# A hybrid Hyena and attention encoder layer: convolutions in two stages, attention chained behind its hyena, an early first operand

## The chip, the cores and the metric

The kernel runs on one core of one Trainium2 chip. The metric is the device time of one execution in microseconds (us). The time before is 3018.79 us, the median of 3 runs (3017.01 to 3024.18).

## The reference

Two independent sequences (prompt, s = 0, and sample, s = 1) of T = 1024 tokens with model width D = 1024 go through one encoder layer in fp32, with a final RMS norm.

```python
h = rmsnorm(x, norm1_g)
u_h, q, k, v, g_h, g_a = split(h @ w_in)        # 1536, 512, 128, 128, 1024, 1024
y_h = hyena_mixer(u_h, ...)                     # z = gate * (fftconv(z, filt[o]) + bias[o] * z), o = 0, 1
y_a = window_attention(rope(q), rope(k), v)     # blocks of 128, window 128, a sink logit
merged = sigmoid(g_h) * (y_h @ w_up_hyena) + sigmoid(g_a) * (y_a @ w_up_attn)
x = x + merged @ w_out
h = rmsnorm(x, norm2_g)
x = x + (silu(h @ w_ff_gate) * (h @ w_ff_up)) @ w_ff_down
return rmsnorm(x, final_g)
```

There are 8 query heads and 2 key heads of 64, and the feed-forward width is 2816. The convolutions are bidirectional ones of length 2T over 512 channels, two of them (o = 0 and 1) for each sequence.

## The kernel before

**Numbers.** A large product keeps fp32 accuracy by splitting each operand into a high and a low fp32r part (`part`, L338 to L342: ScalarE casts, L341, and VectorE subtracts, L342) and doing three matmuls: high·high, high·low, low·high. In the projections these are L559, L560, L561, in the feed-forward part L1045, L1046, L1047.

**Stages.** `main` runs, for each sequence, the projections that feed the hyena (`proj_u`), q, k and v (`proj_qkv`) and the gates (`proj_gates`), sequence 0 first, all in pool `pa`. Then in pool `pb` come the merges: `merge_up(s, i)`, the hyena's (i = 0) and the attention's (i = 1) up products, weighted by the gates (loads of the intermediate results L917, of the gates L922), and `merge_out`, the product with w_out and the residual. Last come the feed-forward halves `ffn_up` and `ffn_down`, in Strassen form (`strassen`, seven products instead of eight). Before `ffn_up(0)`, `b_side(k)` makes for each of four quarters k of the contraction the seven operands B11, T1, T2, B21, T3, B22, T4 out of the normed rows.

**What runs beside what.** Hyena and attention are a side stream: generators that yield the cost of each step. `mix(main, side, rate)` takes a step of the main stream (10.4 for a column block of a projection, 2.6 or 5.2 for one of a merge) and then side steps until their costs (4.5 for a convolution's group, 5.5 for one of attention's) have used up the main step's cost times the rate. RATES holds the eight rates: projections u, qkv, gates of sequence 0 (0 to 2), of sequence 1 (3 to 5), the merges of sequence 0 (6), and the first operands beside the last merges (7). Filters and hyena(0) lie beside the projections of sequence 0, then attention(0), then hyena(1) beside the later projections of sequence 1. What is left of a side stream when `pa` ends is drained, and attention(1) starts only in `pb`. The order of emission sets each engine's priorities in a scheduler; within one engine instructions run in the order so fixed. SyncE's queue issues the loads and stores in order too.

**A convolution.** `conv` works on 256 channels. It goes through the frequencies in eight groups, four in each of two parts. For a group: a butterfly sum (VectorE, `fwd_butterfly`), the sum As (`both`, L380), the forward transform as matmuls into a PSUM bank (`dft`, L396, L400, L401; L392 for group 0; a copy by ScalarE, L397, between), the load of the filter's spectrum K (L440), the pointwise product on VectorE (t2 L443, t1 L450, their sum L451, the sum Ys L380), the inverse transform on TensorE (`dft` again, or `dft_across`, L418, L424, L425, in the second convolution), and a ScalarE copy to B. After the four groups of a part `inv_even` or `inv_odd` combine B on VectorE (L170 to L215). Line 451 stands once in each group, 64 times in the kernel. `hyena` multiplies by its gates (L477, L484) and writes yh (L485).

**Attention.** `attention(s)` loads kv (L811), rotates it (L802 to L805, L819), transposes it on TensorE (L826), and then per block loads qb (L839), makes scores, softmax and values.

**The feed-forward evacuation.** In `ffn_up` each pass p has a gate half and an up half. In the up half `evac` copies the partial results M1 and M5 to tiles c (tag `yr`, 3 buffers, copy at L1106), adds further products to them (L1111), and multiplies with the gate half (L1096).

Of the kernel before, what the change touches and what calls it, by code (L numbers as in the profile page):

```python
# [19 lines left out]
P = 128  # L20
# [26 lines left out]
RATES = (1.0, 0.85, 1.0, 1.0, 1.1, 1.22, 1.3, 0.3)  # L47
# [77 lines left out]
def bc(ap, n, axis):  # L125
    return ap.unsqueeze(axis).to_broadcast([*ap.shape[:axis], n, *ap.shape[axis:]])
# [91 lines left out]
class Kern:  # L218
# [209 lines left out]
    def conv(self, pool, z, o, h, fm, mf, mi):  # L428
        nc = self.nc
        B = {}  # L430
        y = None

        def tmp(tag, n):
            return pool.tile([P, n, CH], F32, tag=tag, name=tag, bufs=1)

        y = pool.tile([P, 8, CH], F32, tag="z", name="y", bufs=2)
        for part in range(2):
            for g, X in self.spectrum(pool, z, part, mf):
                K = pool.tile([P, 3, CH], F32, tag="K", name="K", bufs=KB)
                nc.sync.dma_start(K, self.kd[o][h][:, g, 0:3])  # L440
                t1 = pool.tile([P, 2, CH], F32, tag="t1", name="t1", bufs=YB)
                t2 = pool.tile([P, 2, CH], F32, tag="t2", name="t2", bufs=1)
                nc.vector.tensor_tensor(t2, X[:, ::-1], K[:, 1:3], ALU.mult)  # L443
                if g == 0:
                    Kd = pool.tile([P, CH], F32, tag="Kd", name="Kd", bufs=1)
                    nc.sync.dma_start(Kd, self.kd[o][h][:, 0, 3])
                    nc.vector.tensor_tensor(t1[:, 0], X[:, 0], K[:, 0], ALU.mult)
                    nc.vector.tensor_tensor(t1[:, 1], X[:, 1], Kd, ALU.mult)
                else:
                    nc.vector.tensor_tensor(t1, X, bc(K[:, 0], 2, 1), ALU.mult)  # L450
                nc.vector.tensor_tensor(t1, t1, t2, ALU.add)  # L451
                ys = self.both(pool, t1, g, "Ys")
                B[g] = pool.tile([P, 2, CH], F32, tag="B", name="B", bufs=4)
                if not fm:
                    nc.scalar.copy(B[g], self.dft("sb", mi[g], t1, ys, g))
                else:
                    nc.scalar.copy(B[g].rearrange("p c (t n) -> p t c n", t=2), self.dft_across("sb", mi[g], t1, ys, g))
# [509 lines left out]
    def b_side(self, tmp, s, k, r, out):  # L967
# [327 lines left out]
    def main(self, outs):  # L1295
# [3 lines left out]
        def drain(g):  # L1299
            for _ in g:  # L1300
                pass
# [31 lines left out]
        with tc.tile_pool(name="pa", bufs=PA, reuse_waits="tile") as pool:  # L1333
# [9 lines left out]
            side = chain(side, self.hyena(1))  # L1343
            side = mix(self.proj_qkv(pool, 1, hs), side, R[4])
            side = mix(self.proj_gates(pool, 1, hs), side, R[5])
            if side:
                drain(side)
        self.arb = 2
        with tc.tile_pool(name="pb", bufs=TB, reuse_waits="tile") as tmp:
            side = self.attention(1)  # L1350
            next(side)
# [3 lines left out]
            with tc.tile_pool(name="ya", bufs=1, reuse_waits="tile") as yp, tc.tile_pool(name="ma", bufs=1, reuse_waits="tile") as pool:  # L1355
# [33 lines left out]
            with tc.tile_pool(name="ff", bufs=1, reuse_waits="tile") as fp:  # L1389
# [3 lines left out]
                drain(self.b_side(tmp, 0, 3, rr[0], hb[0]))  # L1393
# [80 lines left out]
```

## Time and profile before

| what | before |
|---|---|
| median of 3 runs | 3018.79 us |
| profiled execution | 3016.99 us |
| its span | 3015.2 us |
| its mean granted clock | 0.978 |
| TensorE (PE) busy | 2890.0 us, 96% |
| VectorE (DVE) busy | 2113.9 us, 70% |
| ScalarE (ACT) busy | 1231.6 us, 41% |
| DMA | 510.92 MB, mean 169 GB/s |

The profile is of one execution. Its page gives busy times by engine and the chain that ended last; the timeline of an engine lists its instructions with start, duration, line and operation, and in brackets how long the engine had been idle and what ended that. Where a table of stretches is shown, the granted clock is TensorE's, as a share of full speed. A row's busy PE time is of pipelined matmuls, so 0.39 us may stand for one whose successor starts 0.23 us later. By lines, gates(0) lies at about 340 to 563 us, proj_u(1) and proj_qkv(1) from 580 us, gates(1) up to 1146 us, the merges from there to 1697 us, and `ffn_up(0)` from 1697 to 2128 us.

### The profile page before, as it was taken

How to read it: one execution, taken by the hardware profiler on the slowest of the kernel's cores; microseconds unless marked ns; L12 is line 12 of the kernel's file. 1: busy time of each engine (PE TensorE's matmuls, PEld its weight loads, DVE VectorE, ACT ScalarE, POOL GpSimd, SP SyncE). 2: the span in 40 equal slices, each digit the busy share in tenths (PEclk: the TensorE clock that was granted, in tenths of full speed). 3: DMA queues.
4: the chain of work that ended last, by engine and by line, in shares of the span. 5: the costliest groups of instructions: out<-in, count | busy, mean ns of one | idle time of the engine just before them, and what ended most of it. 6: DMA issues, size and time to landing. Idle time of an engine off the chain costs nothing.

```text
span 3015.2 us, 36438 instructions
## 1 busy us (share of the span) xinstructions
PE 2890.0 (96%) x13498; PEld 2349.6 (78%) x13498; DVE 2113.9 (70%) x3437; ACT 1231.6 (41%) x2039; POOL 74.9 (2%) x146
## 2 busy tenths in 40 slices
PE   8999899899999998499999999999999999999998
PEld 6789687677897776377777788888787888888887
DVE  6875787877746677688678567787465666676665
ACT  5334212336752223388554334444112434443122
POOL 0000000000000000000000000000111000001100
PEclk9999899999999999699999999999999999999999
DMA  4455654423253445243676345555866244447642
GB/s 155 155 195 206 226 188 161 148 88 107 72 165 111 131 136 171 87 139 127 187 225 206 116 153 203 216 206 200 313 251 252 97 161 154 153 146 270 263 167 70
DMA packets 202431, 510.92 MB, mean 169 GB/s; under 512 B 19623, under 2 KB 68427, under 8 KB 202253
## 3 DMA queue, kind: packets, MB, share of 16 engines
q1 hardware_dynamic: 182093, 435.18, 42.4%
q0 software_dynamic: 20160, 73.41, 6.2%
q8 instruction: 106, 1.74, 0.2%
q14 instruction: 72, 0.59, 0.1%
HBM read 350.69 MB, written 157.83 MB: 169 GB/s over the span
## 4 chain that ended last, share of the span: by engine, by line
PE 76%; DVE 7%; DMA 3%; ACT 2%; issue 1%; SPq 0%; DVEq 0%; ACTq 0%
PE mm L560 7%; PE mm L559 7%; PE mm L561 7%; PE mm L1045 4%; PE mm L1046 4%; PE mm L1047 4%; PE mm L1242 2%; PE mm L1243 1%; PE mm L1244 1%; PE sc L396 1%; PE sb L1045 1%; PE sd L1045 1%; PE sb L1046 1%; PE sb L1047 1%; PE sd L1046 1%; PE sa L1045 1%
## 5 line engine op out<-in xcount | busy, mean ns | idle before, releaser
L341 ACT CAST whi<-raw 128x1024 fp32r<-128x1024 f32 (+1 forms) x270 | 264.2, 979 | 546.3 <-PE mm L560 199.4
L342 DVE TENSOR_TENSOR wlo<-raw,whi 128x1024 fp32r<-128x1024 f32 (+1 forms) x270 | 305.8, 1134 | 164.6 <-ACT whi L341 163.8
L559 PE MATMUL mm<-hh,whi 128*128 128x512 f32 x824 | 334.1, 405 | 0.1
L560 PE MATMUL mm<-hl,whi 128*128 128x512 f32 x824 | 334.0, 405 | 0.0
L561 PE MATMUL mm<-hh,wlo 128*128 128x512 f32 x824 | 333.3, 404 | 0.0
L341 ACT CAST whi<-s 128x1024 fp32r<-128x1024 f32 x104 | 109.1, 1049 | 256.2 <-PE mm L1046 57.8
L1046 PE MATMUL mm<-r,whi 128*128 128x512 f32 x528 | 206.9, 392 | 1.1 <-DVE r L342 1.1
L1045 PE MATMUL mm<-r,whi 128*128 128x512 f32 x528 | 207.9, 394 | 0.0
L1047 PE MATMUL mm<-r,wlo 128*128 128x512 f32 x528 | 206.6, 391 | 0.0
L559 PEld LDWEIGHTS mm<-hh,whi 128*128 128x128 f32 x824 | 155.7, 189 | 30.3 <-DVE uc L737 0.5
L561 PEld LDWEIGHTS mm<-hh,wlo 128*128 128x128 f32 x824 | 155.4, 189 | 30.4 <-issue 0.5
L560 PEld LDWEIGHTS mm<-hl,whi 128*128 128x128 f32 x824 | 155.5, 189 | 29.9 <-issue 0.7
L342 DVE TENSOR_TENSOR wlo<-s,whi 128x1024 fp32r<-128x1024 f32 x104 | 126.9, 1221 | 14.0 <-ACT whi L341 12.6
L1024 POOL DMA_DIRECT2D r<-comb x112 | 59.4, 530 | 2738.7 <-PE mm L1047 2113.2
L559 PE MATMUL mm<-yh,whi 128*128 128x512 f32 x256 | 106.8, 421 | 12.4 <-ACT yh L341 9.2
L1046 PEld LDWEIGHTS mm<-r,whi 128*128 128x128 f32 x528 | 99.1, 188 | 23.4 <-DVE r L342 1.4
L1047 PEld LDWEIGHTS mm<-r,wlo 128*128 128x128 f32 x528 | 99.1, 188 | 22.6
L1045 PEld LDWEIGHTS mm<-r,whi 128*128 128x128 f32 x528 | 99.3, 188 | 22.4 <-ACT sg L1106 0.2
L767 PE MATMUL mm<-whi,hh 128*128 128x256 f32 x384 | 110.9, 291 | 0.0
L769 PE MATMUL mm<-whi,hl 128*128 128x256 f32 x384 | 110.5, 288 | 0.0
L560 PE MATMUL mm<-yl,whi 128*128 128x512 f32 x256 | 105.5, 413 | 5.0 <-DVE yl L342 4.9
L768 PE MATMUL mm<-wlo,hh 128*128 128x256 f32 x384 | 110.0, 288 | 0.0
(551 smaller groups left out, 7278.2 us busy)
## 6 DMA issues: line engine op xcount, KB each, us to landing
r<-comb POOLq DMA_DIRECT2D x112, 512.0 KB, 9.7
comb<-stage SPq DMA_DIRECT2D x48, 1024.0 KB, 5.2
K<-kd SPq DMA_DIRECT2D x64, 384.0 KB, 3.3
raw<-in_w_fg SPq DMA_DIRECT2D x44, 512.0 KB, 5.6
raw<-in_w_fu SPq DMA_DIRECT2D x44, 512.0 KB, 3.6
raw<-in_w_g SPq DMA_DIRECT2D x32, 512.0 KB, 4.1
gt<-ge SPq DMA_DIRECT2D x32, 512.0 KB, 3.3
raw<-in_w_up SPq DMA_DIRECT2D x32, 512.0 KB, 4.8
```

The costliest lines, as they stand in the source:

```text
L341: self.nc.scalar.copy(hi, src)
L342: self.nc.vector.tensor_tensor(lo, src, hi.bitcast(F32), ALU.subtract)
L559: mm(ps, hi[:, k], xh[:, s], start=(i == 0), stop=False)
L560: mm(ps, hi[:, k], xl[:, s], start=False, stop=False)
L561: mm(ps, lo[:, k], xh[:, s], start=False, stop=(i == n - 1))
L767: nc.tensor.matmul(ps[:, q], xh[:, t], wh, start=(i == 0), stop=False)
L768: nc.tensor.matmul(ps[:, q], xh[:, t], wl, start=False, stop=False)
L769: nc.tensor.matmul(ps[:, q], xl[:, t], wh, start=False, stop=(i == 7))
L1045: mm(ps, hi[:, k], xh, start=(first and k == 0), stop=False, skip_group_check=not first)
L1046: mm(ps, hi[:, k], xl, start=False, stop=False, skip_group_check=not first)
L1047: mm(ps, lo[:, k], xh, start=False, stop=(k == n - 1), skip_group_check=not first)
L1242: mm(ps, hi[:, w], xh, start=(first and q == 0), stop=False, skip_group_check=not first)
```

## The change

Four edits. (1) In `conv` the back half of a group (K's load, pointwise product, inverse transform, copy to B) becomes a function, called when the next group's forward transform has been emitted. (2) Four rates change. (3) attention(1) is chained to hyena(1) in pool `pa`, and what is left of that side stream isn't drained there but goes on beside the merges. (4) `b_side(3)` starts under the last merges: its operand B11 goes to two tiles of tag `yr`, and the rest of it is done where all of it was done.

```diff
-RATES = (1.0, 0.85, 1.0, 1.0, 1.1, 1.22, 1.3, 0.3)
+RATES = (1.0, 1.0, 1.1, 1.1, 1.1, 1.22, 1.0, 0.3)
...
+        def back(g, X):
+            K = pool.tile([P, 3, CH], F32, tag="K", name="K", bufs=KB)
+            nc.sync.dma_start(K, self.kd[o][h][:, g, 0:3])
...
+            nc.vector.tensor_tensor(t2, X[:, ::-1], K[:, 1:3], ALU.mult)
...
+            nc.vector.tensor_tensor(t1, t1, t2, ALU.add)
+            ys = self.both(pool, t1, g, "Ys")
...
         for part in range(2):
-            for g, X in self.spectrum(pool, z, part, mf):
...
-                yield 4.5
+            last = None
+            for got in self.spectrum(pool, z, part, mf):
+                if last:
+                    back(*last)
+                    yield 4.5
+                last = got
+            back(*last)
+            yield 4.5
...
-    def b_side(self, tmp, s, k, r, out):
+    def b_side(self, tmp, s, k, r, out, first=None):
...
-        put("B11", xa[:, 0])
+        if first:
+            got["B11"] = first
+            self.part(*first, xa[:, 0])
+            yield 2.0
+        else:
+            put("B11", xa[:, 0])
...
-            side = chain(side, self.hyena(1))
+            side = chain(side, self.hyena(1), self.attention(1))
             side = mix(self.proj_qkv(pool, 1, hs), side, R[4])
             side = mix(self.proj_gates(pool, 1, hs), side, R[5])
-            if side:
-                drain(side)
         self.arb = 2
         with tc.tile_pool(name="pb", bufs=TB, reuse_waits="tile") as tmp:
-            side = self.attention(1)
-            next(side)
...
                     for k in range(3):
                         yield from self.b_side(tmp, 0, k, rr[0], hb[0])
+                    two = [tmp.tile([P, 512], F32R, tag=YR[0], name="b11", bufs=YR[1]) for _ in range(2)]
+                    self.b3 = self.b_side(tmp, 0, 3, rr[0], hb[0], two)
+                    yield next(self.b3)
...
-                drain(self.b_side(tmp, 0, 3, rr[0], hb[0]))
+                drain(self.b3)
```

In the code after, lines behind `conv` stand 8 further down and lines behind `b_side` 13; in `conv`, K's load is L438, t2 L441, t1 L448, their sum L449. No engine's order differs ahead of the first convolution (some 319 us) or behind `ffn_up(0)`.

What moves is shown at three places. The first is TensorE at the first convolution of hyena(0), whose groups stand beside the end of the projections of sequence 0. L396, L400 and L401 are one transform; dft_f is a forward matrix, dft_i an inverse one. Before:

```order
L392 MATMUL sb<-t_2485,dft_i_2450 128x256 x4
L396 MATMUL sc<-Ys,dft_i_2452 128x256
L400 MATMUL sb<-t_2510,dft_i_2452 128x256
L401 MATMUL sb<-t_2510,dft_i_2452 128x256
L396 MATMUL sc<-As,dft_f_2438 128x256
L400 MATMUL sd<-A,dft_f_2438 128x256
L401 MATMUL sd<-A,dft_f_2438 128x256
L396 MATMUL sc<-Ys,dft_i_2454 128x256
```

After:

```order
L396 MATMUL sc<-As,dft_f_2438 128x256
L392 MATMUL sb<-t_2493,dft_i_2450 128x256 x4
L400 MATMUL sd<-A,dft_f_2438 128x256
L401 MATMUL sd<-A,dft_f_2438 128x256
L396 MATMUL sc<-Ys,dft_i_2452 128x256
L400 MATMUL sb<-t_2523,dft_i_2452 128x256
L401 MATMUL sb<-t_2523,dft_i_2452 128x256
L396 MATMUL sc<-As,dft_f_2440 128x256
```

The forward transform of a group now stands ahead of the inverse transform of the group before it. Further on beside gates(0) the order before has 12 to 23 matmuls of the gates between the pieces of a group and the next; the order after has dense places with 4 matmuls between pieces (8 to 14 to a group), and between these places pauses of 51 to 84. All that is left of hyena(0) at the start of gates(0) ends within it.

The second place is TensorE at the end of hyena(1) and the start of attention(1). L424 and L425 are the last inverse transform, L826 (after: L834) the transposes of kv, L559 to L561 (after: L567 to L569) products. Before:

```order
L424 MATMUL sb<-dft_i_7432,t_9756 128x128
L425 MATMUL sb<-dft_i_7432,t_9756 128x128
L424 MATMUL sb<-dft_i_7432,t_9756 128x128
L425 MATMUL sb<-dft_i_7432,t_9756 128x128
L826 MATMUL sd<-ident,kv 128x128 x4
L826 MATMUL sa<-ident,kv 128x128 x4
L559 MATMUL mm<-yh,whi 128x512
L560 MATMUL mm<-yl,whi 128x512
```

After:

```order
L567 MATMUL mm<-hh_5048,whi 128x512
L568 MATMUL mm<-hl_5049,whi 128x512
L834 MATMUL sd<-ident,kv 128x128 x4
L834 MATMUL sa<-ident,kv 128x128 x4
L569 MATMUL mm<-hh_5048,wlo 128x512
L567 MATMUL mm<-hh_4992,whi 128x512
L568 MATMUL mm<-hl_4993,whi 128x512
L569 MATMUL mm<-hh_4992,wlo 128x512
```

The transposes stood directly behind the last inverse transform, among the merges' products (yh); they now stand among those of the gates (hh), and 112 matmuls of the gates lie between the last inverse transform and them. Of attention(1) some part lies in the end of the gates, some 31 of its matmuls stand at the passage to the merges with no product among them, and the rest lies beside the first merges. On SyncE's queue the write of yh stands ahead of the load of kv before and after; after, the gates' writes (L797, which was L789) stand around them.

The third place is ScalarE in an up half of `ffn_up(0)`. L1106 (after: L1119) copies a partial result to c, L341 casts weights. Before:

```order
L1098 ACTIVATE sg<-mm 128x512
L1106 COPY c<-sb 128x512
L1106 COPY c<-sa 128x512
L341 CAST whi<-raw 128x512
L1106 COPY c_14630<-sb 128x512
```

After:

```order
L1119 COPY c<-sb 128x512
L341 CAST whi<-raw 128x512
L1119 COPY c_14631<-sb 128x512
L341 CAST whi<-raw 128x1024
L1119 COPY c<-sa 128x512
```

The copy of the bank sa to c moves behind the casts, since its tile comes free later.

More of the change, by code (lines that the diff above doesn't have):

```diff
@@ L434, in tmp @@
             return pool.tile([P, n, CH], F32, tag=tag, name=tag, bufs=1)
+        def back(g, X):
+            K = pool.tile([P, 3, CH], F32, tag="K", name="K", bufs=KB)
+            nc.sync.dma_start(K, self.kd[o][h][:, g, 0:3])
+            t1 = pool.tile([P, 2, CH], F32, tag="t1", name="t1", bufs=YB)
+            t2 = pool.tile([P, 2, CH], F32, tag="t2", name="t2", bufs=1)
+            nc.vector.tensor_tensor(t2, X[:, ::-1], K[:, 1:3], ALU.mult)
+            if g == 0:
+                Kd = pool.tile([P, CH], F32, tag="Kd", name="Kd", bufs=1)
+                nc.sync.dma_start(Kd, self.kd[o][h][:, 0, 3])
+                nc.vector.tensor_tensor(t1[:, 0], X[:, 0], K[:, 0], ALU.mult)
+                nc.vector.tensor_tensor(t1[:, 1], X[:, 1], Kd, ALU.mult)
+            else:
+                nc.vector.tensor_tensor(t1, X, bc(K[:, 0], 2, 1), ALU.mult)
+            nc.vector.tensor_tensor(t1, t1, t2, ALU.add)
+            ys = self.both(pool, t1, g, "Ys")
+            B[g] = pool.tile([P, 2, CH], F32, tag="B", name="B", bufs=4)
+            if not fm:
+                nc.scalar.copy(B[g], self.dft("sb", mi[g], t1, ys, g))
+            else:
+                nc.scalar.copy(B[g].rearrange("p c (t n) -> p t c n", t=2), self.dft_across("sb", mi[g], t1, ys, g))
@@ L436, in conv @@
         y = pool.tile([P, 8, CH], F32, tag="z", name="y", bufs=2)
         for part in range(2):
-            for g, X in self.spectrum(pool, z, part, mf):
[L439 to L457, printed above, removed]
-                yield 4.5
@@ L977, in put @@
             got[name] = (t[:, 0], t[:, 1])
-        put("B11", xa[:, 0])
+        if first:
+            got["B11"] = first
+            self.part(*first, xa[:, 0])
+            yield 2.0
+        else:
+            put("B11", xa[:, 0])
         tt(xa[:, 0], xa[:, 1], xa[:, 0], ALU.subtract)
```

## The prediction

> **What bounds the kernel now.** The first view is the page: busy time by engine, and the chain of waits that ended last.
>
> ```profile
> span 3015.2 us, 36438 instructions
> ...
> PE 2890.0 (96%) x13498; PEld 2349.6 (78%) x13498; DVE 2113.9 (70%) x3437; ACT 1231.6 (41%) x2039; POOL 74.9 (2%) x146
> ...
> PE 76%; DVE 7%; DMA 3%; ACT 2%; issue 1%; SPq 0%; DVEq 0%; ACTq 0%
> ...
> K<-kd SPq DMA_DIRECT2D x64, 384.0 KB, 3.3
> ```
>
> TensorE is the bound, and no edit takes a matmul away. So what can be won is PE's idle time and the slow matmuls behind it. The second view cuts the span into stretches, by the granted clock. Columns: stretch, length, busy time (and instructions) of PE, weight loads, DVE, ACT, POOL; granted clock; DMA share; GB/s.
>
> ```profile
> 319.00:345.00 26.00, 14.76 (x37) 9.30 (x37) 18.17 (x25) 12.22 (x16) 0.00 (x0) 0.67 0.71 235
> 345.00:563.00 218.00, 217.92 (x994) 175.55 (x994) 169.57 (x274) 50.99 (x81) 0.00 (x0) 1.00 0.52 178
> 580.00:598.00 18.00, 6.86 (x23) 4.91 (x21) 17.45 (x30) 3.65 (x6) 0.00 (x0) 0.62 0.17 59
> 631.00:640.00 9.00, 5.51 (x18) 3.85 (x17) 7.63 (x15) 1.84 (x3) 0.00 (x0) 0.81 0.03 12
> 697.00:708.00 11.00, 5.57 (x24) 4.24 (x24) 9.76 (x29) 5.95 (x13) 0.00 (x0) 0.69 0.00 1
> 850.00:1146.00 296.00, 295.59 (x1477) 241.91 (x1476) 181.85 (x314) 91.89 (x165) 0.00 (x0) 1.00 0.42 139
> 1146.00:1163.00 17.00, 8.98 (x27) 6.33 (x26) 16.90 (x25) 5.90 (x9) 0.00 (x0) 0.70 0.71 246
> 1206.00:1292.00 86.00, 45.05 (x162) 32.45 (x162) 59.89 (x139) 32.64 (x70) 0.00 (x0) 0.65 0.27 86
> 1230.31:1240.59 10.28, 6.19 (x19) 4.30 (x19) 2.40 (x4) 1.73 (x3) 0.00 (x0) 0.50 0.01 2
> 1292.00:1454.00 162.00, 159.16 (x787) 123.99 (x785) 139.97 (x380) 141.93 (x325) 0.00 (x0) 0.99 0.43 136
> 1454.00:1462.00 8.00, 4.16 (x10) 2.73 (x10) 6.99 (x12) 4.06 (x7) 0.00 (x0) 0.79 0.58 176
> 1697.00:1708.00 11.00, 5.27 (x15) 3.60 (x15) 10.80 (x21) 6.88 (x9) 0.00 (x0) 0.69 0.18 54
> ```
>
> I count a stretch's loss as length minus PE busy time × clock, which takes in both idleness and slowness. In order of time: 16.1 (319:345), 13.7 (580:598), 4.5 (631:640), 7.2 (697:708), 10.7 (1146:1163), 56.7 (1206:1292), 4.4 (1292:1454), 4.7 (1454:1462) and 7.4 us (1697:1708). That is 125 us within the change's reach; beside gates in 345:563 and 850:1146 convolutions cost nothing. The largest loss, by PE's timeline:
>
> ```profile
> 1240.59 1.19 PE L418 MATMUL sc<-dft_i,Ys 128*128 128x128 f32 x4 [2.71 <-DVE Ys L380]
> ...
> 1243.93 0.63 PE L425 MATMUL sb<-dft_i,t 128*128 128x128 f32 x2
> 1267.41 1.11 PE L826 MATMUL sd<-ident,kv 128*128 128x128 f32 x4 [22.85 <-DVE kv L805]
> ```
>
> A group with nothing beside it takes a period of 10.28 us at clock 0.50 (the row 1230.31:1240.59), and behind the last one PE stands for 22.85 us until attention's keys are there. Three rows tell why, DVE's first, then SyncE's queue:
>
> ```profile
> 1253.79 2.29 DVE L484 TENSOR_TENSOR gx<-gx,y 128x2048 f32<-128x2048 f32 x1
> ```
>
> ```profile
> 1256.11 0.38 SPq L485 DMA_DIRECT2D yh<-gx  x1
> 1256.58 0.53 SPq L811 DMA_DIRECT2D kv<-qkv  x1
> ```
>
> The inverse transform's last sums and the product L484 run first, the hyena's write waits for L484, and the load of kv is queued behind that write though it doesn't need it.
>
> **The change part by part.** The sum is made against the profiled execution, 3016.99 us; the median shown, 3018.79, is 1.8 above, so I add the sum to the median.
>
> *Attention chained behind its hyena (and rate 6, 1.3 to 1.0).* All of hyena(1) moves ahead of the end of gates(1), and by the order 112 gate matmuls stand between its last transform and the transposes of kv. Their pace, and the change of pools behind the gates:
>
> ```profile
> 1146.14 0.39 PE L560 MATMUL mm<-hl,whi 128*128 128x512 f32 x1
> 1146.37 0.40 PE L561 MATMUL mm<-hh,wlo 128*128 128x512 f32 x1
> 1154.64 1.22 PE L559 MATMUL mm<-yh,whi 128*128 128x512 f32 x2 [7.88 <-ACT yh L341]
> ```
>
> At 0.23 us from start to start, 112 matmuls take 25.8 us, against a wait of 22.85. The kv load, the write of yh ahead of it in SP's queue and the gate writes L789 that now come between fit into that cover, barely; without it 22.85 us come back. The bare groups get matmuls beside them too. Of 56.7 I leave 6: **−51**. At 1146:1163 the 7.88 us are the load and cast of the merge's first operand. Attention's matmuls now stand around that place, but the order shows some 31 of them with no product beside them, and they wait for exponentials themselves. So half: **−5** (0 to −9). Merge products that had attention beside them until 1454 run with less of it; the end at 1454:1462 (a wait for a split operand) goes mostly, **−2.7**, and I give back **+3** (0 to 6) for attention's own waits in fewer products.
>
> *Two-stage convolution.* Per group nothing is added on PE, DVE or ACT. K's load (3.3 us to landing by the page) moves with the product; its two buffers come free one product earlier than needed, and a bare period is three times that long, so zero. Where groups stand bare, the next group's forward matmuls fill the wait for Ys: at 319:345 half of 16.1, **−8** (−3 to −12; there the chip also loads, DMA share 0.71).
>
> *Rates 1, 2 and 3.* By the order all that is left of hyena(0) now lies beside gates(0). The groups, by the stretches of line 451 (one a group):
>
> ```profile
> 345.00:563.00 218.00, 12.33 (x18) 1.00 0.52 178
> 345.00:708.00 363.00, 19.21 (x28) 0.97 0.45 148
> ```
>
> So 28 groups instead of 18. DVE's other rows of gates(0) are L786 (first) and L342 (second); the third is L342 beside hyena(1):
>
> ```profile
> 345.00:563.00 218.00, 20.57 (x30) 1.00 0.52 178
> ...
> 345.00:563.00 218.00, 22.28 (x22) 1.00 0.52 178
> 850.00:1146.00 296.00, 23.19 (x19) 1.00 0.42 139
> ```
>
> A group costs DVE (169.57 − 20.57 − 22.28) / 18 = 7.0 us with its inverse. With 28 groups that is 197 + 43 = 240 us of DVE. PE has 218 plus ten groups of at most 6.19 × 0.50 = 3.1 us (the bare row): at most 249. DVE is then 96% full or more, where it was 78%, and it serves in order. Here the gain is paid for. In a dense place by the order, a group stands with 8 to 14 products: PE needs 2.3 (estimate; overlapping records make 3.1 too much) to 3.1 us and 14 × 0.23 at most, 4.2 to 6.3 in all; DVE needs 2.40 (bare row), a half-width and two full-width rows of a butterfly (12.33 / 18 = 0.69 a full one), 4.1 in all, and 43 / 28 = 1.5 for the gates: 5.6. The wait lies between 0 and 1.4 us; 0.8 because PE is nearer to its lower figure. 28 × 0.8 = **+22** (0 to 39). Beside gates(1), whose results ACT copies out, DVE has only 23.19 / 32 = 0.7 beside the 4.1: 0.2 each for 32 groups, **+6** (0 to 20).
>
> What this buys: no groups are left in 580:708. At 580:598 PE waits for DVE:
>
> ```profile
> 592.63 0.48 PE L747 MATMUL tr<-ident,uc 128*128 128x128 f32 x1 [8.18 <-DVE uc L737]
> ```
>
> DVE had 17.45 of 18 us of work, the inverse sums among it. That wait goes; the first tile's own time through DVE stays: **−7** of 13.7. At 631:640 it is a group's wait: **−4.5**. At 697:708 attention(0) ends with nothing beside it; it ends earlier now, beside proj_u(1): **−2** of 7.2.
>
> *B11 early.* ffn_up's first product waits for its operands' casts at the stage's start:
>
> ```profile
> 1703.69 0.79 PE L1045 MATMUL sd<-r,whi 128*128 128x512 f32 x1 [4.61 <-ACT whi L341]
> ```
>
> The two loads, two scalings and one split of k = 3 move under the merge's last products: **−4** of 7.4 (0 to −6). The price: the two yr tiles are held through ffn_up(0), so one of three is left for c. In the up passes M5's copy then waits for M2's product L1096, whose tile it takes. DVE first, then PE, then ACT's copy:
>
> ```profile
> 1887.09 0.69 DVE L1096 TENSOR_TENSOR sg<-sg,c 128x512 f32<-128x512 f32 x1
> ```
>
> ```profile
> 1887.66 0.39 PE L1045 MATMUL mm<-r,whi 128*128 128x512 f32 x1
> ```
>
> ```profile
> L1106 ACT COPY c<-mm x27: 580/588/589, 1760.9 to 2724.0; 128x512 f32<-128x512 f32 x27
> ```
>
> L1096 ends at 1887.78 and the copy takes 0.59, so the bank that the matmul of 1887.66 needs is free at 1888.37 instead: 0.7 us late. Five of the eleven passes are placed like this, the others have room: **+4** (0 to 10).
>
> The sum: −51 − 5 − 2.7 − 8 − 7 − 4.5 − 2 − 4 = −84, and 3 + 22 + 6 + 4 = +35; −49 in all, 2970 us on the median. What matters most is one number, the mean wait w of a group over 60 groups: the time is 3018.8 − 84 + 7 + 60w, with w = 28/60 = 0.47 in my sum.
>
> **The rivals.**
>
> *Groups hardly wait* (w from 0 to 0.1, and half or none of the 7): pieces of the next transform are ready before they are needed, and DVE's queue recovers in the pauses of 51 to 84 products that the order shows between dense places. −75 to −84, 2935 to 2944. For it: 217.92 of 218 us busy at 78% of DVE. Against: 96%.
>
> *DVE becomes the bound* (w about 1, from 0.8 to 1.3): 18 us more in a queue that is already full, whose late results also hold the gates' banks. −84 + 7 + 60 = −17, 3002 us.
>
> *The tail stays uncovered:* the kv load lies in SP's queue behind the write of yh still, and the order puts the cover in a place where a late L484 eats it; 22.85 us and some slow matmuls, 25 in all, come back: 2995 us. This is the case in which the move does not do what it says.
>
> *Thin cover, slower:* by the order, only four matmuls (4 × 0.23 = 0.92 us) stand between two pieces in the dense places of gates(0). The chain from a forward result through L441, the product, the sum and Ys is 2.40 us of DVE with all else queued ahead. If each group stops PE for 2 us, the sum is −84 + 7 + 120 = +43: 3062. It decides from w = 1.28 upwards. Against it: a bare group, with nothing at all beside it, waits 2.71 us for Ys (the row 1240.59); 0.92 us of products and half of the next transform now stand in that place.
>
> *The clock:* if those many short stops lower the granted clock over all of gates(0) to the 0.67 of 319:345, 241 us of products take 241 / 0.67 = 360, 119 more: 3089. The row 1292:1454 speaks against it, 2.8 us idle in small pieces at clock 0.99. The Trainium skill has such a rule on its page "TensorE: Matmul & The Clock Gate", section "A second HAM failure mode: psum-queue depth-cycling": frequent micro-idles between groups of matmuls can make the clock swing between half and full. By that rule this change would lose; the trace so far does not bear it out.
>
> **How the numbers follow.** My forecast (w between 0.2 and 0.8, all else as summed) has 0.55: 2970, with 2954 to 2990 as its own range. Groups hardly waiting 0.20, DVE bound 0.12, uncovered tail 0.05, thin cover 0.04, clock 0.02, and 0.02 for something unnamed that eats the gain. The range 2933 to 3005 leaves out the slow end of the DVE case (0.05), thin cover, clock, the unnamed, and a little below: 0.16. A measurement of this kernel tells about 0.3% from no change, 9 us. Faster by more: 0.55 + 0.20 + 0.05 + two thirds of 0.12 = 0.88; within it the rest of that case and the unnamed, 0.06; slower 0.06.
>
> **What would show it.** In the profile after, the stretch behind hyena(1) should have no PE wait over 5 us at the kv transposes, and the clock between the gates and the merge's middle should be over 0.95. In gates(0) the DVE should be over 93% busy, and PE's idle time there some 20 us, put down to DVE's Ys and t. There should be no conv group behind gates(0), and at the start of proj_u(1) no wait of 8 us. In ffn_up(0) there should be waits of 0.7 us for ACT's copy in about five passes. I am wrong if gates(0) has under 6 us of such waits (then the time is about 2950 or less) or over 50 (then above 2995), or if the wait for kv is still over 15 us.

## The result and the profile after

The changed kernel takes 2943.31 us (median of 4 runs, 2938.68 to 2945.47), the kernel before 3020.78 us beside it (4 runs, 3017.01 to 3024.18). The ratio is 0.9742, with a 95% interval of 0.9724 to 0.9759. The forecast was 2970 us, a gain of 49 us; the gain is 77. That lies inside the stated range, and by its size it is the rival in which groups hardly wait.

The page of the changed kernel, busy times and the chain that ended last:

```profile
span 2941.1 us, 36418 instructions
...
PE 2871.4 (98%) x13498; PEld 2341.1 (80%) x13498; DVE 2114.2 (72%) x3437; ACT 1232.8 (42%) x2040; POOL 74.9 (3%) x146
...
PE 86%; DVE 7%; ACT 3%; DMA 3%; issue 1%; SPq 0%; DVEq 0%; ACTq 0%
```

The work is the same (DVE 2114.2 against 2113.9 us); PE is idle for less. The stretches that answer to those shown of before, in the same columns (gates(0) of this kernel has its last product at 590.6 us, where that of the kernel before has it at about 557):

```profile
319.00:345.00 26.00, 10.16 (x34) 6.15 (x32) 21.18 (x33) 10.48 (x14) 0.00 (x0) 0.72 0.62 210
345.00:365.00 20.00, 18.29 (x80) 14.47 (x81) 17.54 (x34) 5.95 (x10) 0.00 (x0) 0.85 0.33 119
365.00:570.00 205.00, 204.53 (x954) 166.09 (x953) 184.81 (x300) 47.45 (x74) 0.00 (x0) 1.00 0.52 175
570.00:600.00 30.00, 27.28 (x139) 21.43 (x139) 24.95 (x42) 13.01 (x22) 0.00 (x0) 1.00 0.56 184
600.00:625.00 25.00, 21.24 (x81) 16.57 (x81) 19.03 (x43) 12.94 (x22) 0.00 (x0) 0.80 0.50 169
625.00:690.00 65.00, 62.98 (x314) 48.69 (x313) 54.29 (x172) 50.23 (x123) 0.00 (x0) 0.97 0.29 85
860.00:1110.00 250.00, 248.86 (x1322) 208.90 (x1321) 194.31 (x316) 73.47 (x120) 0.00 (x0) 1.00 0.40 130
1110.00:1150.00 40.00, 40.00 (x191) 33.16 (x191) 22.20 (x50) 12.32 (x20) 0.00 (x0) 1.00 0.42 145
1150.00:1170.00 20.00, 19.71 (x100) 14.73 (x99) 16.16 (x56) 15.11 (x41) 0.00 (x0) 1.00 0.21 67
1170.00:1290.00 120.00, 109.16 (x509) 83.67 (x508) 102.87 (x286) 108.40 (x251) 0.00 (x0) 0.94 0.41 129
1290.00:1400.00 110.00, 109.08 (x503) 87.33 (x502) 77.65 (x145) 65.37 (x122) 0.00 (x0) 1.00 0.61 190
1620.00:1632.00 12.00, 9.64 (x45) 7.99 (x44) 11.82 (x19) 9.75 (x14) 0.00 (x0) 0.81 0.31 112
```

With the formula of the prediction (a stretch's loss is its length minus PE's busy time × clock) the losses compare like this, in us:

| place | before | after | change | forecast |
|---|---|---|---|---|
| start of gates(0) (319:345 and 345:365) | 16.1 | 18.7 + 4.5 | +7.1 | −8 |
| groups beside gates(0) | 0.1 | 0.5 | +0.4 | +22 |
| proj_u(1) and attention(0) | 13.7 + 4.5 + 7.2 | 2.7 + 8.0 + 3.9 | −10.8 | −13.5 |
| groups beside gates(1) | 0.4 | 1.1 | +0.7 | +6 |
| from the end of the gates to the end of attention(1) | 10.7 + 56.7 + 4.4 + 4.7 | 0 + 0.3 + 17.4 + 0.9 | −57.9 | −55.7 |
| start of `ffn_up(0)` | 7.4 | 4.2 | −3.2 | −4 |
| within `ffn_up(0)` | 0.4 | 0.2 (420.75 us busy of 421 at 1632:2053) | −0.2 | +4 |

That is 64 of the 74 us by which the span is shorter; the other 10 lie in stretches not listed and in the formula, which is rough where matmuls overlap. PE's waits of the changed kernel, the costliest:

```profile
PE mm L567 <- DVE ge L794: 12.1, 1, 12.1
PE mm L581 <- ACT whi L341: 7.7, 2, 7.0
PE sc L904 <- ACT ph L349: 3.9, 4, 1.6
```

No wait for a group's Ys or t is among them; the longest for Ys is 1.88 us, at 330.64 us, and beside gates(0) PE loses 0.5 us in all. The wait of 22.85 us for kv is gone: PE's timeline has products from the last inverse transform at 1120.33 up to the transposes, and none of these rows has a wait.

```profile
1120.33 0.39 PE L425 MATMUL sb<-dft_i,t 128*128 128x128 f32 x2
...
1146.07 0.66 PE L834 MATMUL sd<-ident,kv 128*128 128x128 f32 x4
```

The longest wait is now one of 12.1 us at the start of gates(0): PE waits for VectorE to take a gate product out of its PSUM bank (the evacuation, into the tile ge, L794):

```profile
346.71 0.80 PE L567 MATMUL mm<-hh,whi 128*128 128x512 f32 x1 [12.08 <-DVE ge L794]
```

What holds the gates back there is older than the change. In the kernel before, the gates' products pause from 316.70 to 342.53 us, behind a ge that starts at 340.06 (after: from 317.55 to 346.71, behind a ge at 345.97):

```profile
340.06 1.28 DVE L786 TENSOR_TENSOR ge<-mm,rf 128x512 f32<-128x512 f32 x2
```

```profile
342.53 0.99 PE L559 MATMUL mm<-hh,whi 128*128 128x512 f32 x1
```

Before, the pause is filled by bare groups with shorter waits; after, the groups end at 334.6 us and PE stands.

### The profile page after: what moved, and what is told of

It is laid out like the page before. It is cut to its first block, busy times and chain, and to the rows that moved or that the text cites. A ratio compares the mean times of both kernels' runs of the same rounds, so it can differ in the third digit from the quotient of the medians.

```text
span 2941.1 us, 36418 instructions
## 1 busy us (share of the span) xinstructions
PE 2871.4 (98%) x13498; PEld 2341.1 (80%) x13498; DVE 2114.2 (72%) x3437; ACT 1232.8 (42%) x2040; POOL 74.9 (3%) x146
## 4 chain that ended last, share of the span: by engine, by line
PE 86%; DVE 7%; ACT 3%; DMA 3%; issue 1%; SPq 0%; DVEq 0%; ACTq 0%
PE mm L567 8%; PE mm L568 8%; PE mm L569 8%; PE mm L1058 4%; PE mm L1059 4%; PE mm L1060 4%; PE sc L396 2%; PE mm L1255 1%; PE mm L1256 1%; PE mm L1257 1%; PE sd L1058 1%; PE sb L1058 1%; PE sb L1059 1%; PE sb L1060 1%; PE sd L1059 1%; PE sd L1060 1%
## 5 line engine op out<-in xcount | busy, mean ns | idle before, releaser
L341 ACT CAST whi<-raw 128x1024 fp32r<-128x1024 f32 (+1 forms) x270 | 264.3, 979 | 595.3 <-PE mm L568 208.8
L342 DVE TENSOR_TENSOR wlo<-raw,whi 128x1024 fp32r<-128x1024 f32 (+1 forms) x270 | 306.1, 1134 | 204.0 <-ACT whi L341 203.7
L567 PE MATMUL mm<-hh,whi 128*128 128x512 f32 x824 | 334.3, 406 | 12.1 <-DVE ge L794 12.1
L568 PE MATMUL mm<-hl,whi 128*128 128x512 f32 x824 | 334.6, 406 | 0.0
L569 PE MATMUL mm<-hh,wlo 128*128 128x512 f32 x824 | 333.2, 404 | 0.0
L341 ACT CAST whi<-s 128x1024 fp32r<-128x1024 f32 x104 | 109.1, 1049 | 250.2 <-PE mm L1059 56.8
L1058 PE MATMUL mm<-r,whi 128*128 128x512 f32 x518 | 203.4, 393 | 0.0
L1059 PE MATMUL mm<-r,whi 128*128 128x512 f32 x518 | 202.8, 391 | 0.0
L567 PEld LDWEIGHTS mm<-hh,whi 128*128 128x128 f32 x824 | 155.6, 189 | 40.9 <-DVE ge L794 12.8
L569 PEld LDWEIGHTS mm<-hh,wlo 128*128 128x128 f32 x824 | 155.4, 189 | 28.7 <-issue 0.5
L342 DVE TENSOR_TENSOR wlo<-s,whi 128x1024 fp32r<-128x1024 f32 x104 | 127.0, 1221 | 16.3 <-ACT whi L341 15.4
L567 PE MATMUL mm<-yh,whi 128*128 128x512 f32 x256 | 102.4, 403 | 1.7 <-DVE gin L935 1.6
```

The costliest lines, as they stand in the source:

```text
L341: self.nc.scalar.copy(hi, src)
L342: self.nc.vector.tensor_tensor(lo, src, hi.bitcast(F32), ALU.subtract)
L567: mm(ps, hi[:, k], xh[:, s], start=(i == 0), stop=False)
L568: mm(ps, hi[:, k], xl[:, s], start=False, stop=False)
L569: mm(ps, lo[:, k], xh[:, s], start=False, stop=(i == n - 1))
L1058: mm(ps, hi[:, k], xh, start=(first and k == 0), stop=False, skip_group_check=not first)
```

## The experiments

The numbers are medians; "before" is the kernel before, run between the others on the same chip, and every ratio is to it.

**Which edit carries the gain.** By the prediction the tail is covered since attention is chained behind its hyena (theory B). The other reading (theory A) is that the two-stage convolution carries it. It came from the order of some variants: how many of TensorE's 13498 matmuls stand ahead of the last transform of hyena(1), and ahead of the transposes of kv behind it. Counted in the traces:

| kernel | ahead of the last transform | ahead of the transposes of kv |
|---|---|---|
| before | 5912 | 5913 |
| change | 5559 | 5672 |
| change, one-stage convolution | 5912 | 5913 |
| change, attention in pb | 5559 | 5745 |
| before, two-stage convolution | 5569 | 5745 |

First, the three other edits without the two-stage convolution (the edit against the changed kernel):

```diff
-            last = None
-            for got in self.spectrum(pool, z, part, mf):
-                if last:
-                    back(*last)
-                    yield 4.5
-                last = got
-            back(*last)
-            yield 4.5
+            for g, X in self.spectrum(pool, z, part, mf):
...
+                yield 4.5
```

> The changed kernel with the convolution in one stage as before (the three other edits stay). In this kernel's order TensorE's convolution pieces stand almost where they stood before the change: hyena(1) ends directly ahead of the transposes of kv, with no product between. Theory A (the two-stage convolution is what lets hyena(1) end earlier; rates and chain only use that): the 22.85 us wait and the bare groups come back, 3008 to 3022 us. Theory B, that of the prediction (chaining attention behind the hyena covers the tail, the convolution edit is worth some 8 us): 2950 to 2965 us.

Measured: 3016.4 us, ratio 0.998 (0.9971 to 0.9989). All but some 6 us of the gain is gone, and the tail stands in PE's timeline as it did before:

```profile
1239.83 1.20 PE L418 MATMUL sc<-dft_i,Ys 128*128 128x128 f32 x4 [2.71 <-DVE Ys L380]
...
1266.65 1.12 PE L826 MATMUL sd<-ident,kv 128*128 128x128 f32 x4 [22.83 <-DVE kv L805]
```

Chain, rates and early B11 together are worth little without the convolution. Then the chain alone (with its rate) taken back, in the changed kernel:

```diff
-RATES = (1.0, 1.0, 1.1, 1.1, 1.1, 1.22, 1.0, 0.3)
+RATES = (1.0, 1.0, 1.1, 1.1, 1.1, 1.22, 1.3, 0.3)
...
-            side = chain(side, self.hyena(1), self.attention(1))
+            side = chain(side, self.hyena(1))
...
+            if side:
+                drain(side)
...
+            side = self.attention(1)
+            next(side)
```

> The changed kernel with attention(1) back in pool pb, what is left of the side stream drained at the end of pa, and rate 6 back at 1.3. Theory A: hyena(1) still ends 185 products ahead of the transposes of kv, so most of the tail stays covered; the load of kv starts at the pool change and stands bare for some 5 to 15 us: 2950 to 2965 us. Theory B: the tail comes back, 2990 to 3000 us.

Measured: 2939.48 us, ratio 0.9729 (0.9714 to 0.9743), the same as the whole change or a little better. Both theories expected a longer time. Attention's first load does stand bare, but for one wait only:

```profile
PE sd L868 <- issue: 5.9, 1, 5.9
```

The 5.9 us (qb's transposes) are new, and in exchange the waits for ph (L904, 3.9 us in the changed kernel) are not among the costliest. The counter-test, the two-stage convolution alone on the kernel before:

```diff
         for part in range(2):
-            for g, X in self.spectrum(pool, z, part, mf):
...
+            last = None
+            for got in self.spectrum(pool, z, part, mf):
+                if last:
+                    back(*last)
+                    yield 4.5
+                last = got
+            back(*last)
+            yield 4.5
```

> The kernel before with the two-stage convolution alone (old rates, attention in pool pb, B11 not early). Theory A (this edit is the cause): 2932 to 2945 us, all of the gain or more. Theory B (chaining attention and the rates carry the gain): 3000 to 3012 us.

Measured: 2934.48 us, ratio 0.972 (0.9704 to 0.9735). One edit has the whole gain; the three others together add nothing to it. Theory B falls.

**The rates.**

```diff
-RATES = (1.0, 1.0, 1.1, 1.1, 1.1, 1.22, 1.0, 0.3)
+RATES = (1.0, 0.85, 1.0, 1.0, 1.1, 1.22, 1.0, 0.3)
```

> The changed kernel with the rates 1 to 3 back at 0.85, 1.0, 1.0. By the order hyena(1) ends at the same place (111 products ahead of the transposes). Theory A: 2940 to 2952 us, a few us of waits at the start of proj_u(1) back, the 12.1 us wait for the gates' evacuation at the start of gates(0) perhaps gone. Theory of the prediction's terms (DVE-bound gates(0) costs 22 us, less with the old rates, against 13 us won behind it): 2934 us, faster by 9.

Measured: 2934.49 us, ratio 0.9707 (0.9691 to 0.9724): the old rates are better, by some 9 us. The number is the one that the terms of the prediction gave, and theory A's range was missed, but the reason isn't the one that those terms gave (a full DVE beside gates(0)). The stretches of this kernel from gates(0) on:

```profile
365.00:570.00 205.00, 204.19 (x947) 165.53 (x945) 174.49 (x279) 46.11 (x72) 0.00 (x0) 1.00 0.52 177
570.00:600.00 30.00, 27.73 (x134) 22.07 (x134) 28.30 (x48) 14.15 (x25) 0.00 (x0) 1.00 0.63 220
600.00:625.00 25.00, 23.72 (x119) 19.02 (x118) 19.48 (x35) 8.95 (x14) 0.00 (x0) 1.00 0.24 81
625.00:690.00 65.00, 64.88 (x328) 51.73 (x327) 52.72 (x146) 41.52 (x88) 0.00 (x0) 1.00 0.41 127
```

Beside gates(0) nothing is won (0.8 us lost here, 0.5 in the changed kernel). What is won lies at 600:690: 1.3 + 0.1 us lost instead of 8.0 + 3.9. With the faster rates hyena(0) ends earlier (its last group's sum is at 582.8 us, with the old rates at 612.7), and attention(0)'s start falls on the start of proj_u(1), where PE waits for kv (2.58 us at 617.26) and for splits of its own operands (L342, 2.05 us at 599.02 the longest).

**B11.** The edit is taken back:

```diff
-                    two = [tmp.tile([P, 512], F32R, tag=YR[0], name="b11", bufs=YR[1]) for _ in range(2)]
-                    self.b3 = self.b_side(tmp, 0, 3, rr[0], hb[0], two)
-                    yield next(self.b3)
...
-                drain(self.b3)
+                drain(self.b_side(tmp, 0, 3, rr[0], hb[0]))
```

> The changed kernel with b_side(3) whole at the start of ffn_up again, no tiles of yr held. If the term of 4 us for the earlier operand is right and the squeeze of yr costs nothing (as the changed kernel's trace shows in ffn_up(0)): slower by 2 to 4 us, 2945 to 2948. If neither matters: 2943.

Measured: 2945.35 us, ratio 0.975 (0.9736 to 0.9765). The 2 us are in the right direction, but the intervals overlap. PE's list of waits has the old one of the first product of ffn_up(0) back:

```profile
PE sd L1058 <- ACT whi L341: 4.6, 1, 4.6
```

Against 2.36 us in the changed kernel.

**Why groups don't wait.** Two more DVE rows in each group's chain (line 441's product is written three times; the values stay the same):

```diff
             nc.vector.tensor_tensor(t2, X[:, ::-1], K[:, 1:3], ALU.mult)
+            nc.vector.tensor_tensor(t2, X[:, ::-1], K[:, 1:3], ALU.mult)
+            nc.vector.tensor_tensor(t2, X[:, ::-1], K[:, 1:3], ALU.mult)
```

> The changed kernel with line 441's multiply written three times instead of once, two more DVE rows of 0.69 us in each group's chain (the values are the same). DVE in 365:570 would go from 184.8 to 184.8 + 22 x 1.37 = 215 us of 205. If DVE stands 1.3 us of row time from being the bound of a group (its queue takes the sums of the butterflies in the pauses, and a dense place lasts four groups): slower by 20 to 45 us, most of it beside gates(0). If every group were as near to a wait as the prediction's 0.8 us took it to be: 64 x 1.37 = 88 us slower. If buffers and pauses absorb it: under 10 us.

Measured: 2964.46 us, ratio 0.9816 (0.9794 to 0.9838): 21 us slower than the change, at the low end of the first case, but not where it was expected. The stretches:

```profile
365.00:570.00 205.00, 203.35 (x929) 164.75 (x928) 180.23 (x289) 46.29 (x72) 0.00 (x0) 1.00 0.52 176
570.00:600.00 30.00, 24.04 (x89) 17.45 (x88) 28.18 (x49) 10.11 (x17) 0.00 (x0) 0.89 0.43 152
600.00:625.00 25.00, 18.76 (x95) 15.22 (x94) 23.93 (x43) 8.52 (x14) 0.00 (x0) 0.93 0.37 111
625.00:690.00 65.00, 61.62 (x309) 49.28 (x308) 53.60 (x104) 24.04 (x38) 0.00 (x0) 1.00 0.38 118
```

and the groups by stretch (one sum each), first of this kernel (L451 here), whose gates(0) ends at 570.5 us, then of the changed kernel up to the end of its gates(0) (L449):

```profile
345.00:570.00 225.00, 13.87 (x20) 0.98 0.50 169
570.00:700.00 130.00, 5.51 (x8) 0.95 0.37 119
```

```profile
345.00:591.00 246.00, 19.16 (x28) 0.99 0.50 171
```

Beside gates(0) PE loses 1.7 us. DVE is no fuller there (180.2 against 184.8 us at 365:570): 20 groups lie beside gates(0) and 8 behind it, where the changed kernel has all 28 beside it. Behind, 570:690 loses 8.6 + 7.6 + 3.4 = 19.6 us against 14.6. More is lost further on, first of this kernel, then of the changed one:

```profile
690.00:860.00 170.00, 164.77 (x922) 136.79 (x921) 131.97 (x408) 135.97 (x329) 0.00 (x0) 0.98 0.22 68
1170.00:1290.00 120.00, 103.36 (x461) 78.26 (x460) 105.58 (x261) 83.61 (x180) 0.00 (x0) 0.93 0.49 162
```

```profile
690.00:860.00 170.00, 169.47 (x925) 138.46 (x924) 118.85 (x307) 108.53 (x241) 0.00 (x0) 1.00 0.37 119
```

That is 8.5 us against 0.5 at 690:860 and 23.9 against 17.4 at 1170:1290. So of the 21 us some 1 is lost beside gates(0) and the rest behind it. A longer chain is answered here by a later place in the order, not by a wait in the same place. That also means that this run does not show what a fuller DVE beside gates(0) would have cost.

**The wait of 12.1 us.** The gates' evacuation (ge, L794) is what PE waits for. DVE's order in the changed kernel has six of the seven sums of squares of sequence 1's norm (L638, from `norm_stats`) ahead of it. Squares, rows and ge share the tag t4, a ring of 5 buffers. First, these statistics moved into the gates' steps (the late statistics, below):

```diff
-            r1 = self.norm_stats(pool, xT[1])
-            side = mix(beside(self.proj_gates(pool, 0, hs), self.prenorm(pool, xT[1], r1)), side, R[2])
+            side = mix(beside(self.proj_gates(pool, 0, hs), self.prenorm(pool, xT[1])), side, R[2])
...
-    def prenorm(self, pool, src, r):
+    def prenorm(self, pool, src):
...
-        r = self.spread_dma(pool, r)
+        acc = pool.tile([P, T], F32, tag="ar", name="acc", bufs=self.arb)
+        for k in range(KC):
+            x = pool.tile([P, T], F32, tag="t4", name="xin")
+            self.nc.sync.dma_start(x, src[k])
+            self.square_sum(pool, acc, x, k == 0)
+            if k % 2:
+                yield
+        r = self.spread_dma(pool, self.norm_scale(pool, acc))
```

> The changed kernel with the statistics of sequence 1's norm moved into the gates' steps, two row blocks to a step, so that the gates' first results don't need a buffer (tag t4, 5 of them) that the squares of these statistics hold. If the 12.1 us wait of TensorE at 334.6 us comes from this ring of buffers (in the order the gates' first evacuation stands behind six of the seven sums of squares): the wait falls under 3 us and with it some of the 20.5 us at half clock, 2925 to 2932 us. If it comes from the transforms that DVE does first there: 2940 to 2945 us.

Measured: 2933.34 us, ratio 0.9718 (0.97 to 0.9735). The wait is gone altogether, the first row; so where the statistics stand decides it. But some 10 us are won and not the 23.2 that 319:365 lost, for behind the gates, which now end at 557 us, losses grew:

```profile
319.00:345.00 26.00, 26.00 (x115) 20.88 (x114) 23.36 (x38) 12.03 (x17) 0.00 (x0) 1.00 0.71 250
...
365.00:570.00 205.00, 201.56 (x939) 162.89 (x937) 183.61 (x302) 54.37 (x87) 0.00 (x0) 0.99 0.56 193
570.00:600.00 30.00, 24.46 (x120) 19.19 (x118) 27.89 (x49) 10.63 (x18) 0.00 (x0) 0.91 0.20 62
600.00:625.00 25.00, 19.51 (x86) 15.40 (x87) 18.21 (x46) 9.83 (x16) 0.00 (x0) 0.83 0.51 169
```

These rows lose 5.5, 7.7 and 8.8 us, against 0.5, 2.7 and 8.0 in the changed kernel; 625:690 loses 3.9 less.

The same with the statistics moved the other way, ahead of `proj_qkv(0)`:

```diff
+            r1 = self.norm_stats(pool, xT[1])
             side = mix(self.proj_qkv(pool, 0, hs), side, R[1])
...
-            r1 = self.norm_stats(pool, xT[1])
```

> The changed kernel with the statistics of sequence 1's norm emitted ahead of proj_qkv(0), so that they are done before the gates begin. Ring of buffers as the cause of the 12.1 us wait: the wait goes, 2925 to 2932 us, unless the ring now stops proj_qkv(0). Transforms on DVE as the cause: 2940 to 2945 us.

Measured: 2937.94 us, ratio 0.9732 (0.9716 to 0.9749): between the two ranges. The wait leaves gates(0), and one nearly as long comes up at 227.43 us, in the filters' transforms (PE's waits, 10.7 us the longest):

```profile
PE sd L392 <- DVE A L139: 13.6, 3, 10.7
```

Both moves take the wait out of gates(0). By what means the statistics held ge back is not shown. In the changed kernel's trace DVE works without a pause from 335.33 us up to ge, 3.4 us on three sums of squares and 7.2 us on the convolution's sums, which all stand ahead of ge in its order:

```profile
345.97 0.68 DVE L794 TENSOR_TENSOR ge<-mm,rf 128x512 f32<-128x512 f32 x1
```

That the order has ge there because its tile comes out of the ring that the squares hold is a reading of the code; no run gave ge a ring of its own.

And the late statistics on the kernel before, with its one-stage convolution:

```diff
-            r1 = self.norm_stats(pool, xT[1])
-            side = mix(beside(self.proj_gates(pool, 0, hs), self.prenorm(pool, xT[1], r1)), side, R[2])
+            side = mix(beside(self.proj_gates(pool, 0, hs), self.prenorm(pool, xT[1])), side, R[2])
...
-    def prenorm(self, pool, src, r):
+    def prenorm(self, pool, src):
```

> The kernel before, one-stage convolution and all, with the statistics of sequence 1's norm moved into the gates' steps. Before the change, too, three groups stand with no product beside them at 319:345 and lose 17 us. If the ring of buffers holds the gates back there too: those go, some come back behind the gates, since more of hyena(0) moves there by the order: 3000 to 3010 us. If the bare groups stand there for the one-stage convolution's own chain: 3014 to 3022 us, and the moved statistics are of use only with the two-stage convolution.

Measured: 3019.7 us, ratio 1.0002 (0.9992 to 1.0011). Both cases were wrong in half. The bare groups at 319:345 do go (26.00 us of 26.00 busy), and nothing is won, because losses grow in two other places. This kernel first, then the kernel before at the end of hyena(1):

```profile
319.00:345.00 26.00, 26.00 (x114) 20.74 (x114) 18.16 (x28) 12.44 (x16) 0.00 (x0) 1.00 0.69 243
365.00:570.00 205.00, 199.51 (x902) 159.92 (x900) 160.09 (x255) 51.62 (x84) 0.00 (x0) 0.98 0.53 185
1190.00:1290.00 100.00, 48.96 (x175) 34.98 (x174) 63.16 (x142) 30.02 (x60) 0.00 (x0) 0.64 0.22 70
```

```profile
1190.00:1290.00 100.00, 57.88 (x227) 42.55 (x225) 71.92 (x158) 37.98 (x76) 0.00 (x0) 0.71 0.30 96
```

At 365:570, which now holds the passage to proj_u(1), 205 − 199.51 × 0.98 = 9.5 us are lost (before 0.1), and at 1190:1290 100 − 48.96 × 0.64 = 68.7 (before 58.9). The gates(1) products end 20 us earlier, at 1126 instead of 1146 us, but the last inverse transform of hyena(1) stands at 1246 us, where it stood at 1244: the side stream is no shorter and has fewer products beside it.

**A version that beats the change.** Late statistics with the old rates, first with nothing but the two-stage convolution (the edit against the kernel before):

```diff
+            last = None
+            for got in self.spectrum(pool, z, part, mf):
+                if last:
+                    back(*last)
...
+    def prenorm(self, pool, src):
```

> The kernel before with the two-stage convolution alone, and with the statistics of sequence 1's norm moved into the gates' steps. The two-stage convolution alone took 2934.5; its start of gates(0) still lost 21.8 us, which the moved statistics took away in the changed kernel, where half came back at the start of proj_u(1), since the faster rates had left no group beside it. With the old rates groups still stand there: 2914 to 2922 us. If the loss at proj_u(1) comes from the late statistics and not from the rates: 2924 to 2930.

Measured: 2912.2 us, ratio 0.9649 (0.9635 to 0.9662), somewhat better than expected. Then with chain and early B11 (again against the kernel before):

```diff
-RATES = (1.0, 0.85, 1.0, 1.0, 1.1, 1.22, 1.3, 0.3)
+RATES = (1.0, 0.85, 1.0, 1.0, 1.1, 1.22, 1.0, 0.3)
...
+            side = chain(side, self.hyena(1), self.attention(1))
...
+                    self.b3 = self.b_side(tmp, 0, 3, rr[0], hb[0], two)
```

> The same with attention(1) chained and B11 early (all of the change but the rates 1 to 3, and the statistics moved). Chain and B11 together were worth nothing beside the two-stage convolution (2934.5 both ways): the same as the kernel without them within 4 us.

Measured: 2912.27 us, ratio 0.9647 (0.9633 to 0.966), the same as without them, as expected. Last, with early B11 but attention in pb (against the kernel just measured):

```diff
-RATES = (1.0, 0.85, 1.0, 1.0, 1.1, 1.22, 1.0, 0.3)
+RATES = (1.0, 0.85, 1.0, 1.0, 1.1, 1.22, 1.3, 0.3)
...
-            side = chain(side, self.hyena(1), self.attention(1))
+            side = chain(side, self.hyena(1))
...
+            if side:
+                drain(side)
...
+            side = self.attention(1)
+            next(side)
```

> The same with B11 early, but attention(1) in pool pb (two-stage convolution, B11, statistics moved, old rates). B11 was worth some 2 us: 1 to 4 us below the kernel with the convolution alone and the moved statistics.

Measured: 2907.94 us, ratio 0.9632 (0.9618 to 0.9645): 110 us below the kernel before, some 35 below the change. Its stretches, from the start of gates(0):

```profile
319.00:345.00 26.00, 26.00 (x115) 21.05 (x114) 23.26 (x37) 11.71 (x16) 0.00 (x0) 1.00 0.70 252
345.00:365.00 20.00, 20.00 (x89) 15.93 (x88) 19.28 (x33) 8.43 (x14) 0.00 (x0) 1.00 0.52 177
365.00:570.00 205.00, 201.73 (x936) 163.16 (x935) 182.77 (x300) 54.03 (x86) 0.00 (x0) 0.98 0.56 193
570.00:600.00 30.00, 28.72 (x146) 23.34 (x145) 25.32 (x44) 12.45 (x21) 0.00 (x0) 0.95 0.31 97
600.00:625.00 25.00, 25.00 (x118) 20.19 (x117) 20.48 (x38) 8.52 (x12) 0.00 (x0) 1.00 0.54 183
```

The losses at 319:365 are zero here and small at 570:625 (2.7 us and none); 365:570 loses 7.3. The three best differ by no more than the width of their intervals, so that chain against pool pb stays open at this size.

## Why the prediction was right, and where it was not

**The tail.** The sum gave −55.7 us from the gates' end to the end of attention(1), and the table of losses has −57.9. The 112 products cover the load of kv as worked out. What failed is the step that named the cause, "Attention chained behind its hyena (and rate 6, 1.3 to 1.0). All of hyena(1) moves ahead of the end of gates(1)": with the chain and one-stage groups hyena(1) keeps its place, with 5912 matmuls ahead of its end, and the 22.83 us are there; with two-stage groups and no chain they are not. The two-stage convolution, which the prediction put at −8 us, is worth the whole gain by itself (2934.48 us). The prediction read a row of the whole change's order as the effect of the edit nearest to it. Its number for the tail could come true all the same, since the forecast was for all four edits together; it was no test of the cause. That the two-stage group shortens what the order reckons with, and that groups are therefore placed earlier, is a reading of the five orders in the table above; the time of each is shown.

**Groups beside gates(0), +22, measured +0.4.** This is the term that was mis-sized most. Its count was right: all 28 groups lie beside gates(0) (345:591, shown above). But DVE is 89% busy there (218.30 of 246 us), not 96%, and PE hardly waits. The working put all that DVE does for a group into its dense place: "a half-width and two full-width rows of a butterfly". In the trace most of those rows run in the pauses: of 95 us of them at 365:570, 27 start in dense places, counted as places with at most 14 products between two pieces of groups (116 of the 205 us). Nor did a wait for each group show when each got two more rows: PE loses 1.7 us beside gates(0), and 8 groups move behind it. With it falls the +6 beside gates(1) (+0.7). The two terms were 27 us too dear. The prediction had named this sign itself: under 6 us of such waits means that it is wrong there. Of its other signs the wait for kv, the groups behind gates(0) and the wait of 8 us at proj_u(1) came out as said; the clock at 1170:1290 was 0.94 and not over 0.95.

**The bare groups at 319:345, −8, measured +7.1.** The two-stage groups do run closer: the wait for Ys there shrinks from 3.68 to 1.88 us at the longest. But the step took the gates' products for ready, and in both kernels they are held back by ge, 12.08 us of it now with PE idle. Late statistics take the wait away.

**Rates.** The prediction gave the rates all ten groups by which gates(0) has more (28 instead of 18). Six of them come with the convolution alone: on the kernel before with nothing but the two-stage convolution 24 groups lie beside gates(0), which ends there at 580.4 us (L449):

```profile
345.00:581.00 236.00, 16.53 (x24) 0.98 0.52 175
```

The gain at proj_u(1), −13.5, was −10.8, and it isn't due to the rates: with the old rates that place loses 2.3 + 1.3 + 0.1 = 3.7 us, with the new ones 14.6. By themselves they cost some 9 us.

**B11.** −4 was −3.2 by the rows, 2 us by the times. The price for holding two yr tiles, +4, is about zero. The copy waits for L1109 as predicted, on ACT's timeline:

```profile
1813.78 0.59 ACT L1119 COPY c<-mm 128x512 f32<-128x512 f32 x1 [1.89 <-DVE sg L1109]
```

but the step "the bank that the matmul of 1887.66 needs" failed: its counterpart starts at 1813.64, before this copy and without a wait, so it doesn't need the bank that the copy frees.

**The rivals.** Groups hardly waiting was right in mechanism and size (2935 to 2944). Three others are out by the same rows: PE loses 0.5 us at 365:570, at clock 1.00, so neither DVE's queue nor a thin cover nor a lowered clock cost anything there. The uncovered tail is out since no wait is left at the transposes of attention(1). The rule on micro-idles (the Trainium skill, "TensorE: Matmul & The Clock Gate", section "A second HAM failure mode: psum-queue depth-cycling") had nothing to act on beside gates(0), where PE hardly idled; at 1170:1290, where attention's short waits are, the granted clock is 0.94.

**The sum.** It came out on the right side by its largest term, which stood under the wrong edit, and inside the range partly by luck, since errors of both signs met: groups 27 us and yr some 4 us too dear, the start of gates(0) 15 us too good. Another 10 us of the gain are in no row of the table and in no term.

## What to carry to other kernels

Before a gain is credited to an edit, look at the order with that edit alone: here one edit of four moves everything, and the orders of single edits show it. In this kernel, whose order a scheduler fixes, a shorter or longer chain in each group showed up as a different place of the groups, and the time was won or lost further on, not where the longer or shorter chain stood. And when PE waits for an evacuation, look at what stands ahead of it in the evacuating engine's order, and at who shares the ring of its tile; moving that work is worth a trial, but only with something to cover what follows (the same move was worth 0 us with one-stage groups, and with two-stage ones some 22 at the old rates and some 10 at the new).

## What the runs showed that was not expected

A removed loss was given back at another place: with the late statistics on the kernel before entirely (17 us at 319:345, back at 365:570 and 1190:1290), and with the early ones in large part (a wait of 12.1 us, back as one of 10.7 in the filters' transforms). DVE at 90% of a stretch of 205 us went with a loss of 0.5 us on PE.
